# Splitting w_out earlier, its second half in the first half's places, and two row blocks begun ahead

## The chip, the cores and the metric

The kernel runs on one core of a Trainium2 chip. The metric is the device time of one execution in microseconds (us). Engines are named as in the profile: PE (TensorE matmul), PEld (its weight loads), DVE (VectorE), ACT (ScalarE), POOL (GpSimd) and SP (SyncE, which issues most of the DMAs).

## What is computed

One layer of a hybrid trunk over 1152 tokens (1024 latents and 128 context tokens, nine blocks of 128 rows), width 1024. Three mixers work side by side on parts of one input projection: a Fourier mixer (256 columns), an mLSTM (384) and an S5 scan whose output goes through a GLU (384). Their outputs are laid side by side, 1024 wide, and multiplied by w_out (1024 x 1024); then come a gated residual, a norm, a SwiGLU feed-forward layer and a last norm. Cut to what matters here:

```python
out = jnp.concatenate([f_out, m_out, s_out], axis=-1) @ p["w_out"]
x = x + g1 * out
xn = rmsnorm(x, p["norm2_w"]) * (1 + sc2) + sh2
ff = (jax.nn.silu(xn @ p["w_gate"]) * (xn @ p["w_up"])) @ p["w_down"]
```

## The kernel before, in words

**Products in three.** Each large product is made of three PE instructions (`mm3`, L243): both operands are cut into a high part (a copy that ACT rounds, `split`, L264) and a low part (the difference, made by DVE or POOL). A weight must be loaded, copied by ACT and subtracted by DVE or POOL before PE can use it.

**The order of the work.** Streams (Python generators) hand out instructions. `Weaver.run` (L200) holds a model of each engine's clock and, when the program is built, always emits the instruction that can start earliest by that model; between equal ones the stream's number decides, the lower first. A step marked `VP` goes to DVE or POOL, whichever would end first by the model. So every engine's queue has a fixed order, made from estimated costs, and a stream that waits for a name in `done` waits only for that name's instructions to be emitted. All compute instructions have the line L146 (`emit`), so the trace is read by tiles.

**The output projection.** w_out is used in eight units, each the rows of two of the eight 128-row parts (k) and 512 of the columns: units 0 to 3 make the first half of the columns (j = 0), units 4 to 7 the second (j = 1). `raw_feed` (L1426) loads a unit (512 KB) into one of two buffers `fraw`, `wout_feed` (L1436) splits it into a place `wo0` to `wo7`. Places 0 and 1 are in the pool woA, which is there from the GLU on; 2 to 4 are in woM, opened when the Fourier stream is done; 5 to 7 in woB, opened when the mLSTM's `front` stream and the first half's evacuation (`x0evac`) are done, in the room that these leave. Both streams are added only there where the mLSTM chunks start (L1958 and L1959), behind the GLU and the mLSTM states. After w_out, the two buffers take the feed-forward weights.

`out_project` (L1454) goes through j = 0 and then j = 1. For a row block c, `begin(c)` does the Fourier and GLU parts (k = 0 to 4, 15 PE instructions), and the rest of the block does the mLSTM parts (k = 5 to 7, 9 instructions) when chunk c of the mLSTM has given its output (`m{c}`). In the first half `begin(c + 1)` stands ahead of the rest of block c, so that PE has work while a chunk is made; the last block has none behind it. In the second half the blocks go one after another. One block takes one of the eight PSUM banks from its begin to its evacuation (`evac_x0`, L1519, and `evac_x1`, L1538).

Beside it run `mlstm_front` (L1331) and `mlstm_back` (L1370), chunk by chunk: loads of q, k, v and of a broadcast row `nb`; a mask; exponentials on ACT; products on PE; a norm; a transpose; and the split into MT. The GLU (`glu`, L1116), the mLSTM states (`mlstm_states`, L1175) and the Fourier mixer (`fourier`, L1214, `v_store`, L1291) come before or overlap.

After the second half's blocks, the norm (`norm_scale`, `norm_turned`, `norm_h0`, `norm_h1`, L1555 to L1607) makes operands for the Strassen products of the feed-forward layer. `new` (L1615) and `unit_of` (L1571) put these operands (T1 to T4 and b22) into the places 0 to 7 that w_out has left.

Of the kernel before, what the change touches and what calls it, by code (L numbers as in the profile page):

```python
# [111 lines left out]
class Weaver:  # L112
# [47 lines left out]
    def has(self, *names):  # L160
        return lambda: all(n in self.done for n in names)
# [59 lines left out]
def tile_trunk(ctx, tc, I, O, dbg=None):  # L221
# [13 lines left out]
    def pool(stack, name, bufs=1, side=None):  # L235
        return Pool(wv, stack.enter_context(tc.tile_pool(name=name, bufs=bufs, side=side, reuse_waits="tile")), bufs)
# [1054 lines left out]
    def v_store(fp):  # L1291
        wv.fed["pv"] = [[], 0]
        for _ in range(8):
# [3 lines left out]
            give(pv)  # L1297
            yield Q.dma_start(v_d[:, cl], vt)

    MF = []  # L1300
    sg = ctx.enter_context(ExitStack())
    gp = pool(sg, "glu")
    with ExitStack() as sy:
        yp = pool(sy, "yT")
        add("gluw", glu_weights(gp, yp), 3)
        add("yTfeed", glu_load(yp), 4)
        add("glufeed", glu_feed(yp), 5)
        add("glu", glu(gp), 6)
        add("prep", mlstm_prep(pool(sy, "prep")), 4)
        run("proj", "ada")  # L1310
        swb.close()
        sada.close()

        so_, sf_ = ctx.enter_context(ExitStack()), ctx.enter_context(ExitStack())
        L5["woA"] = pool(so_, "woA", side="right")
        four = pool(sf_, "four", side="right")
        add("vstore", v_store(four), 28)
        add("fourier", fourier(four), 30)
        run("prep", "glufeed")
# [103 lines left out]
    ssh = const.tile([128, 2, NT], F32, name="ssh")  # L1423
    Y, YP, R2 = {}, [], {}

    def raw_feed():  # L1426
        yield has("araw1")

        def make(src):
            raw = raws.tile([128, 1024], F32, name="fraw")  # L1430
            yield Q.dma_start(raw.rearrange("p (k c) -> p k c", k=2) if len(src.shape) == 3 else raw, src)
            return raw
        yield from feed("fraw", [I["w_out"][2 * k:2 * k + 2, :, 512 * j:512 * j + 512].rearrange("k p c -> p k c") for j in range(2) for k in range(4)] + [I[n][i, h].rearrange("p k d j -> p (k d j)") for i in range(NG)
                    for n in ("w_gate", "w_up") for h in range(2)], make, RAWS)

    def wout_feed():  # L1436
        def make(u):
            raw = yield from take("fraw")
            if u >= WOA:
                yield has("woB" if u > WOM else "woM")  # L1440
            t = wo_unit(u, f"wo{u}")
            hi, lo = t[:, 0:D], t[:, D:2 * D]
            yield from split(raw, hi, lo, VP)
            used("fraw")
            return [x.rearrange("p (k c) -> p k c", k=2) for x in (hi, lo)]
        return feed("wout", range(8), make, 8)


    def wo_unit(k, name):
        p = L5["woA" if k < WOA else "woB" if k > WOM else "woM"]  # L1450
        return p.tile([128, 2 * D], F32R, name=name, tag=f"wo{k}")


    def out_project():  # L1454
        for j in range(2):
            ws, po = [], {}

            def mm(c, ks):
                b, i = divmod(c, 3)
                cs = slice(i * 128, (i + 1) * 128)  # L1460
                for k in ks:
                    if len(ws) <= k // 2:
                        ws.append((yield from take("wout")))
                    m = [(MF[b][n][:, (k + 2) % 5] if k < 5 else MT[b][n][:, k - 5])[:, cs] for n in range(2)]
                    w = [x[:, k % 2] for x in ws[k // 2]]
                    yield mm3(po[c], *m, *w, k == 0, k == 7)
                    if c == 8 and k % 2:
                        done.add(f"wo{4 * j + k // 2}")
                    if j and c == 8 and k == 4:
                        done.add("obf")  # L1470

            def begin(c):
                yield lambda c=c: len(MF) > c // 3
                po[c], = yield from bank([128, 512], keep=0 if j else 2)
                yield from mm(c, range(3))
                yield has(f"mf{c // 3}")
                yield from mm(c, range(3, 5))
            if j == 0:
                yield has("vstore")
                yield from begin(0)  # L1480
            for c in range(NT):
                if j:
                    yield from begin(c)
                elif c + 1 < NT:
                    yield from begin(c + 1)
                yield has(f"m{c}")
                yield from mm(c, range(5, 8))
                x1_banks[c, j] = po.pop(c)
                if j and c % 3 == 2:
                    done.add(f"ob{c // 3}")  # L1490
        done.add("out")

    def halved(c, j):
# [75 lines left out]


    def unit_of(i, name):  # L1571
        yield has(f"wo{i}")
        return wo_unit(i, name).rearrange("p (k t) -> p k t", k=4)


# [31 lines left out]
    def norm_h1():  # L1607
        yield has("norm_h0")
        KS = range(4)
        part = {q: [[u[:, k] for u in Y[q]] for k in KS] for q in ("11", "21")}  # L1610

        def f(q, k):
            return [u.bitcast(F32) for u in part[q][k]]

        def new(q, *at):  # L1615
            us = []
            for n, i in enumerate(at):
                us.append((yield from unit_of(i, f"{q}{n}")))
            Y[q] = us
            part[q] = [[u[:, k] for u in us] for k in KS]  # L1620
        b12 = []
        for k in KS:
            b12.append((yield from take("nx")))
            d = xw.tile([128, 512], F32, name="xd", bufs=2)
            yield tt(VP, d, b12[k], f("11", k)[0], ALU.subtract)
            yield tt(VP, d, d, f("11", k)[1], ALU.subtract)
            if k == 0:
                yield from new("T1", 0, 1)
            yield from split(d, *part["T1"][k], VP)
        done.add("T1")  # L1630
        b22 = None
        for k in KS:
            yield has(f"b22{k}")
            b22 = L5["b22"]
            if k == 0:
                yield has("obf")
                Y["22"] = [unit("f", 2, n, "y2", (4, 512)) for n in range(2)]
            yield from split(b22[:, k], *[u[:, k] for u in Y["22"]], VP)
        done.add("22")

        for k in KS:
            yield tt(VP, b12[k], b22[:, k], b12[k], ALU.subtract)
            d = xw.tile([128, 512], F32, name="xd", bufs=2)
            yield tt(VP, d, b12[k], f("11", k)[0], ALU.add)
            yield tt(VP, d, d, f("11", k)[1], ALU.add)
            if k == 0:
                yield from new("T2", 5, 6)
                yield from new("T3", 3, 4)
            yield from split(d, *part["T2"][k], VP)
            yield from split(b12[k], *part["T3"][k], VP)  # L1650
            yield tt(VP, b12[k], f("21", k)[0], d, ALU.subtract)
            if k == 3:
                done.update(("T2", "T3"))
            yield tt(VP, b12[k], b12[k], f("21", k)[1], ALU.add)
        yield from new("T4", 7, 2)
        for k in KS:
            yield from split(b12[k], *part["T4"][k], VP)
        done.add("T4")
# [11 lines left out]
    NG = NFF // 2  # L1670
    WOA, WOM = 2, 4
    GROUPS = [(0, 3), (3, 6), (6, 9), (9, 11)]


# [272 lines left out]
    with ExitStack() as sm_:  # L1947
        mw = pool(sm_, "mw")

        for n, shape, k in (("mt0", [128, 3, 128], 1), ("mt1", [128, 3, 128], 1), ("og", [128, 3, 128], 2), ("nu0", [128, H, 97], 1),  # L1950
                            ("nu1", [128, H, 97], 1), ("h", [128, H, 96], 2), ("xh", [128, 512], 3), ("gt", [128, 512], 2), ("g1", [128, 512], 1),
                            ("va", [128, H, 97], 3), ("qc", [96, H, 128], 3), ("kc", [96, H, 128], 2), ("nb", [128, H, 128], 2),
                            ("P0", [128, H, 128], 2), ("P1", [128, H, 128], 2)):
            mw.place(shape, F32, n, k)
        add("front", mlstm_front(mw), 0)
        add("xhfeed", xh_feed(mw), 19)
        add("x0evac", evac_x0(mw), 9)
        add("fraw", raw_feed(), 24)  # L1958
        add("woutfeed", wout_feed(), 25)  # L1959
        add("out", out_project(), 40)  # L1960
        run("fourier")
        sf_.close()
        L5["woM"] = pool(so_, "woM", side="right")
        done.add("woM")
        run("front", "x0evac")
# [394 lines left out]
```

## Time and profile before

| | |
|---|---|
| median of 3 runs | 1444.98 us (1444.38 to 1445.21) |
| the profiled execution's own time | 1445.23 us |
| its span in the trace | 1443.4 us |
| PE busy | 1350.3 us (94% of the span), granted clock 0.973 in the mean |
| PEld busy | 1113.9 us (77%) |
| DVE, ACT, POOL busy | 941.0 us (65%), 532.3 us (37%), 260.6 us (18%) |
| DMA queue of SP | 116180 packets, 195.44 MB |

The span is the time between the first and the last instruction that the profiler saw; the execution's own time is 1.8 us longer, for what lies around it. A busy PE is not PE at its best: its instructions overlap (a row's duration is longer than the distance to the next start), and its clock has two levels, 1.2 and 2.4 GHz; a granted clock of 1.00 means 2.4 GHz for the whole stretch, 0.5 would be 1.2. In a timeline row the bracket tells how long the engine stood before the instruction, and which instruction's end let it go on. A DMA-issuing instruction is listed under SPq; its data land later.

### The profile page before, as it was taken

How to read it: one execution, taken by the hardware profiler on the slowest of the kernel's cores; microseconds unless marked ns; L12 is line 12 of the kernel's file. 1: busy time of each engine (PE TensorE's matmuls, PEld its weight loads, DVE VectorE, ACT ScalarE, POOL GpSimd, SP SyncE). 2: the span in 40 equal slices, each digit the busy share in tenths (PEclk: the TensorE clock that was granted, in tenths of full speed). 3: DMA queues.
4: the chain of work that ended last, by engine and by line, in shares of the span. 5: the costliest groups of instructions: out<-in, count | busy, mean ns of one | idle time of the engine just before them, and what ended most of it. 6: DMA issues, size and time to landing. Idle time of an engine off the chain costs nothing.

```text
span 1443.4 us, 19010 instructions
## 1 busy us (share of the span) xinstructions
PE 1350.3 (94%) x6885; PEld 1113.9 (77%) x6885; DVE 941.0 (65%) x1798; ACT 532.3 (37%) x1059; POOL 260.6 (18%) x342
## 2 busy tenths in 40 slices
PE   6899999997989889879999999999999999999996
PEld 1787788963968678658788888888888877888885
DVE  5957788975134477736876667766567665535897
ACT  2632232443254443314633333223333324443433
POOL 4364556632215101100000000000000010000011
PEclk9999999998999989989999999999999999999999
DMA  9265422255433865143122222322323339735472
GB/s 325 92 180 147 166 87 82 70 173 169 141 99 96 240 184 168 65 168 118 52 86 81 79 98 89 115 96 72 101 79 115 116 133 379 269 112 195 157 240 95
DMA packets 117682, 199.49 MB, mean 138 GB/s; under 512 B 12364, under 2 KB 53684, under 8 KB 117588
## 3 DMA queue, kind: packets, MB, share of 16 engines
q1 hardware_dynamic: 116180, 195.44, 41.2%
q0 software_dynamic: 1408, 2.83, 0.6%
q8 instruction: 54, 0.88, 0.3%
q14 instruction: 40, 0.33, 0.1%
HBM read 151.77 MB, written 46.47 MB: 137 GB/s over the span
## 4 chain that ended last, share of the span: by engine, by line
PE 71%; DVE 12%; DMA 7%; ACT 3%; issue 3%; POOL 2%; SPq 1%; DVEq 0%; POOLq 0%; ACTq 0%
PE bank L146 71%; DMA fraw<-in_w_ada_dram 3%; DVE xo L146 2%; DMA nb<-nit_d 2%; SPq L146 1%; DVE nu L146 1%; DMA hr<-h_d 1%; DMA v_d<-vt 1%; DVE a L146 1%; DMA out_dram<-cn 1%; DVE bp L146 0%; DVE t L146 0%; ACT P L146 0%; ACT L146 0%; DVE h L146 0%
## 5 line engine op out<-in xcount | busy, mean ns | idle before, releaser
L146 PE MATMUL bank<-ow,oh 128*128 128x512 f32 x912 | 212.9, 393 | 6.0 <-DVE ow L146 5.7
L146 PEld LDWEIGHTS bank<-ow,oh 128*128 128x128 f32 x912 | 172.5, 190 | 43.8 <-DVE ow L146 5.1
L146 PE MATMUL bank<-T,sh 128*128 128x512 f32 x480 | 151.3, 390 | 0.0
L146 DVE TENSOR_TENSOR pu<-pu,bank 128x512 f32<-128x512 f32 x102 | 69.9, 685 | 64.2 <-PE bank L146 64.2
L146 PEld LDWEIGHTS bank<-T,sh 128*128 128x128 f32 x480 | 90.2, 188 | 18.3
L146 POOL TENSOR_TENSOR pu<-pu 128x512 f32<-128x512 f32 x10 | 12.9, 1287 | 475.4 <-DVE pu L146 475.4
L146 PE MATMUL bank<-T,sl 128*128 128x512 f32 x240 | 93.6, 390 | 0.0
L146 DVE TENSOR_TENSOR oh<-hr,oh 128x1536 fp32r<-128x1536 f32 (+2 forms) x29 | 45.3, 1563 | 72.9 <-ACT oh L146 72.9
L146 DVE TENSOR_TENSOR sl<-fraw,sh 128x512 fp32r<-128x512 f32 x40 | 27.7, 693 | 63.4 <-ACT sh L146 62.9
L146 ACT ACTIVATE oh<-hr 128x1536 fp32r<-128x1536 f32 (+2 forms) x29 | 38.4, 1323 | 81.2 <-PE bank L146 55.6
L146 POOL TENSOR_TENSOR y<-ms,nhalf 128x1 f32<-128x1 f32 (+2 forms) x26 | 23.4, 902 | 247.2 <-DVE ms L146 246.3
L146 ACT ACTIVATE sh<-sd 128x512 fp32r<-128x512 f32 x40 | 25.3, 632 | 100.2 <-DVE sd L146 53.4
L146 ACT ACTIVATE pu<-bank 128x512 f32<-128x512 f32 x44 | 26.4, 599 | 88.5 <-PE bank L146 88.3
L146 PE MATMUL bank<-fraw,sc 128*32 128x512 f32 x160 | 46.6, 650 | 11.1 <-DMA fraw<-in_w_ada_dram 11.0
L146 PE MATMUL bank<-T,r20t 128*128 128x512 f32 x160 | 52.8, 391 | 0.0
L146 PEld LDWEIGHTS bank<-T,sl 128*128 128x128 f32 x240 | 45.1, 188 | 8.6
L146 DVE TENSOR_TENSOR_SCAN xo<-dec,ri 64x296 f32<-64x296 f32 x48 | 45.2, 941 | 1.8 <-POOL ri L146 0.7
L146 PE MATMUL bank<-y211f,r20t 128*128 128x512 f32 x96 | 39.4, 410 | 2.6 <-ACT xr L146 2.6
L146 PE MATMUL bank<-y210f,r20t 128*128 128x512 f32 x96 | 38.3, 399 | 0.0
L146 PE MATMUL bank<-y210f,r21t 128*128 128x512 f32 x96 | 38.0, 396 | 0.0
L146 PE MATMUL bank<-y201f,r10t 128*128 128x512 f32 x96 | 37.9, 395 | 0.0
L146 PE MATMUL bank<-y200f,r11t 128*128 128x512 f32 x96 | 37.4, 390 | 0.0
(604 smaller groups left out, 3718.6 us busy)
## 6 DMA issues: line engine op xcount, KB each, us to landing
fraw<-in_w_ada_dram SPq DMA_DIRECT2D x40, 512.0 KB
hr<-h_d SPq DMA_DIRECT2D x21, 768.0 KB
wp<-in_w_down_dram SPq DMA_DIRECT2D x15, 768.0 KB
fraw<-in_w_gate_dram SPq DMA_DIRECT2D x22, 512.0 KB
fraw<-in_w_up_dram SPq DMA_DIRECT2D x22, 512.0 KB
h_d<-sg SPq DMA_DIRECT2D x36, 256.0 KB
wraw<-in_w_feat_dram SPq DMA_DIRECT2D x14, 512.0 KB
h_d<-hs SPq DMA_DIRECT2D x27, 256.0 KB
```

The lines of the kernel that those rows point to most:

```text
L146: s.call(*s.a, **s.k)
```

## The change

The diff does five things. `raw_feed` and `wout_feed` are added before the Fourier streams, beside the GLU (numbers 24 and 25, the Fourier stream has 30), no longer at the mLSTM chunks, and `raw_feed` no longer waits for the name `araw1`. Units 5, 6 and 7 go into the places 0, 1 and 2 once the first half's last row block has read those (`wo0`, `wo1`, `wo2` in `done`), not into woB. `out_project` begins row blocks 0 and 1 of the second half (`begin(0, 1)` and `begin(1, 1)`) after the last `begin` of the first half and ahead of the mLSTM parts of block 8, and block 2 ahead of the rest of block 0; these keep two banks free as the first half does. The places 5 to 7 are used by T1 and T2 alone. T1, T2 and T4 change places with one another, and a table `FREE` says what each place waits for; b22, in place 2, now waits for the last product of the projection.

```diff
+    UNIT = (0, 1, 2, 3, 4, 0, 1, 2)
+    FREE = ("wo5", "wo6", "wo7", "wo3", "wo4", "woB", "woB", "woB")
+    def wo_unit(k, name):
+        p = L5["woA" if k < 2 else "woB" if k > 4 else "woM"]
+        return p.tile([128, 2 * D], F32R, name=name, tag=f"wo{k}")
...
+    def wout_feed():
+        def make(u):
+            raw = yield from take("fraw")
+            if u > 1:
+                yield has(("woM", "woM", "woM", "wo0", "wo1", "wo2")[u - 2])
+            t = wo_unit(UNIT[u], f"wo{u}")
...
         L5["woA"] = pool(so_, "woA", side="right")
+        add("fraw", raw_feed(), 24)
+        add("woutfeed", wout_feed(), 25)
         four = pool(sf_, "four", side="right")
...
     def raw_feed():
-        yield has("araw1")
...
         def make(u):
             raw = yield from take("fraw")
-            if u >= WOA:
-                yield has("woB" if u > WOM else "woM")
-            t = wo_unit(u, f"wo{u}")
...
+        def begin(c, j):
+            yield lambda c=c: len(MF) > c // 3
+            po[c, j], = yield from bank([128, 512], keep=2 if not j or c < 2 else 0)
+            yield from mm(c, j, range(3))
+            yield has(f"mf{c // 3}")
+            yield from mm(c, j, range(3, 5))
+        def end(c, j):
+            yield has(f"m{c}")
+            yield from mm(c, j, range(5, 8))
+            x1_banks[c, j] = po.pop((c, j))
...
+        yield has("vstore")
+        yield from begin(0, 0)
+        for c in range(NT):
+            if c + 1 < NT:
+                yield from begin(c + 1, 0)
+            else:
+                yield from begin(0, 1)
+                yield from begin(1, 1)
+            yield from end(c, 0)
+        for c in range(NT):
+            if c in (0, 3, 4, 5, 6, 7, 8):
+                yield from begin(max(c, 2), 1)
+            yield from end(c, 1)
...
     def unit_of(i, name):
-        yield has(f"wo{i}")
+        yield has(FREE[i])
...
-                yield from new("T1", 0, 1)
+                yield from new("T1", 6, 7)
...
-                yield from new("T2", 5, 6)
+                yield from new("T2", 5, 0)
...
-        yield from new("T4", 7, 2)
+        yield from new("T4", 1, 2)
...
         add("x0evac", evac_x0(mw), 9)
-        add("fraw", raw_feed(), 24)
-        add("woutfeed", wout_feed(), 25)
         add("out", out_project(), 40)
```

## Rows read from the trace of the kernel before

**Rows 1.** Stretches: length, then busy time of each engine (instructions), PE clock, DMA share, GB/s

```profile
398.00:477.00 79.00, 73.13 (x369) 62.28 (x370) 33.03 (x82) 36.90 (x71) 30.94 (x35) 0.96 0.39 96
477.00:530.00 53.00, 40.25 (x245) 34.51 (x243) 32.08 (x71) 24.92 (x73) 2.89 (x3) 0.87 0.78 235
530.00:602.00 72.00, 68.48 (x402) 59.22 (x403) 55.83 (x135) 28.53 (x117) 8.02 (x7) 0.98 0.48 146
611.30:620.50 9.20, 5.92 (x19) 4.10 (x18) 4.31 (x8) 1.24 (x3) 0.00 (x0) 0.79 0.18 59
620.50:635.60 15.10, 7.46 (x22) 5.65 (x23) 5.04 (x6) 3.67 (x5) 0.00 (x0) 0.78 0.81 287
635.60:683.00 47.40, 46.61 (x222) 38.43 (x221) 25.03 (x59) 16.61 (x33) 2.82 (x4) 1.00 0.32 114
697.00:730.00 33.00, 30.44 (x142) 24.97 (x140) 26.67 (x42) 17.35 (x34) 0.00 (x0) 0.95 0.12 39
```

**Rows 2.** Timeline of PE: start, duration, instruction, and what it stood for

```profile
494.95 0.50 PE L146 MATMUL bank<-wo,mf00f 128*128 128x512 f32 x1 [2.95 <-DVE wo L146]
...
613.37 0.52 PE L146 MATMUL bank<-ident,h 128*128 128x128 f32 x3 [2.07 <-DVE h L146]
615.09 0.76 PE L146 MATMUL bank<-wo,mt20t 128*128 128x512 f32 x1 [1.20 <-ACT mt20t L146]
...
623.65 0.50 PE L146 MATMUL bank<-wo,mf00f 128*128 128x512 f32 x1 [3.15 <-DVE wo L146]
...
631.20 0.80 PE L146 MATMUL bank<-wo,mt00t 128*128 128x512 f32 x1 [4.50 <-DVE wo L146]
```

**Rows 3.** Timeline of PE, three products at either level of the clock

```profile
633.08 0.63 PE L146 MATMUL bank<-wo,mt01t 128*128 128x512 f32 x1
633.50 0.63 PE L146 MATMUL bank<-wo,mt00t 128*128 128x512 f32 x1
...
640.19 0.39 PE L146 MATMUL bank<-wo,mf00f 128*128 128x512 f32 x1
640.42 0.39 PE L146 MATMUL bank<-wo,mf01f 128*128 128x512 f32 x1
```

**Rows 4.** Timeline of ACT and DVE: the split of unit 7

```profile
628.83 1.06 ACT L146 ACTIVATE wo<-fraw 128x1024 fp32r<-128x1024 f32 x1 [5.55 <-DMA fraw<-in_w_out_dram]
...
629.92 1.22 DVE L146 TENSOR_TENSOR wo<-fraw,wo 128x1024 fp32r<-128x1024 f32 x1 [5.20 <-ACT wo L146]
```

**Rows 5.** The chain of work that ended last, 477 to 565: start, length, what

```profile
487.14 8.31 DMA nb<-nit_d
...
496.23 1.15 DVE wo L146
497.43 3.50 PE bank L146 x19
...
504.90 6.90 DMA nb<-nit_d
...
516.18 4.82 DMA nb<-nit_d
```

**Rows 6.** DMA view of 477 to 500: all packets, and w_out's loads

```profile
DMA packets 5826, 6.82 MB, mean 296 GB/s; under 512 B 395, under 2 KB 3467, under 8 KB 5825
...
fraw<-in_w_out_dram SPq DMA_DIRECT2D x4, 512.0 KB
```

**Rows 7.** Timeline of DVE and POOL in the GLU's stretch

```profile
471.08 0.56 DVE L146 TENSOR_TENSOR Cst<-dc,Cst 96x388 f32<-96x388 f32 x1 [0.18 <-POOL dc L146]
...
472.51 1.00 POOL L146 TENSOR_TENSOR mf21f<-so,mf20f 128x384 fp32r<-128x384 f32 x1
472.58 1.34 DVE L146 TENSOR_TENSOR Cst<-dc,Cst 96x388 f32<-96x388 f32 x1 [0.94 <-POOL dc L146]
```

**Rows 8.** Timeline of PE: the projection's last product, transposes of rows 4 to 7

```profile
682.77 0.39 PE L146 MATMUL bank<-wo,mt20t 128*128 128x512 f32 x1
...
691.17 1.26 PE L146 MATMUL bank<-ident,xr 128*128 128x128 f32 x10
```

More of the change, by code (lines that the diff above doesn't have):

```diff
@@ L1298, in v_store, with raw_feed, make @@
             yield Q.dma_start(v_d[:, cl], vt)
+    NG = NFF // 2
+    UNIT = (0, 1, 2, 3, 4, 0, 1, 2)
[3 more added lines that the diff above has]
+        return p.tile([128, 2 * D], F32R, name=name, tag=f"wo{k}")
+    def raw_feed():
+        def make(src):
+            raw = raws.tile([128, 1024], F32, name="fraw")
+            yield Q.dma_start(raw.rearrange("p (k c) -> p k c", k=2) if len(src.shape) == 3 else raw, src)
+            return raw
+        yield from feed("fraw", [I["w_out"][2 * k:2 * k + 2, :, 512 * j:512 * j + 512].rearrange("k p c -> p k c") for j in range(2) for k in range(4)]
+                        + [I[n][i, h].rearrange("p k d j -> p (k d j)") for i in range(NG) for n in ("w_gate", "w_up") for h in range(2)], make, RAWS)
+    def wout_feed():
[4 more added lines that the diff above has]
+            t = wo_unit(UNIT[u], f"wo{u}")
+            hi, lo = t[:, 0:D], t[:, D:2 * D]
+            yield from split(raw, hi, lo, VP)
+            used("fraw")
+            return [x.rearrange("p (k c) -> p k c", k=2) for x in (hi, lo)]
+        return feed("wout", range(8), make, 8)
     MF = []
@@ L1424, in tile_trunk @@
     Y, YP, R2 = {}, [], {}
-    def raw_feed():
-        yield has("araw1")
[L1429 to L1434, printed above, removed]
@@ L1436, in wout_feed @@
-    def wout_feed():
-        def make(u):
-            raw = yield from take("fraw")
-            if u >= WOA:
-                yield has("woB" if u > WOM else "woM")
-            t = wo_unit(u, f"wo{u}")
[L1442 to L1451, printed above, removed]
@@ L1454, in out_project @@
-    def out_project():
[L1455 to L1490, printed above, removed]
@@ new lines, in out_project, with mm @@
+    def out_project():
+        ws, po = ([], []), {}
+        def mm(c, j, ks):
+            b, i = divmod(c, 3)
+            cs = slice(i * 128, (i + 1) * 128)
+            for k in ks:
+                if len(ws[j]) <= k // 2:
+                    ws[j].append((yield from take("wout")))
+                m = [(MF[b][n][:, (k + 2) % 5] if k < 5 else MT[b][n][:, k - 5])[:, cs] for n in range(2)]
+                w = [x[:, k % 2] for x in ws[j][k // 2]]
+                yield mm3(po[c, j], *m, *w, k == 0, k == 7)
+                if c == 8 and k % 2:
+                    done.add(f"wo{4 * j + k // 2}")
+                if j and c == 8 and k == 4:
+                    done.add("obf")
+        def begin(c, j):
[8 more added lines that the diff above has]
+            x1_banks[c, j] = po.pop((c, j))
+            if j and c % 3 == 2:
+                done.add(f"ob{c // 3}")
+        yield has("vstore")
[11 more added lines that the diff above has]
+            yield from end(c, 1)
@@ L1668, in norm_p @@
             yield from split(t, *[y[:, k0:k0 + 2] for y in YP], VP)
-    NG = NFF // 2
-    WOA, WOM = 2, 4
     GROUPS = [(0, 3), (3, 6), (6, 9), (9, 11)]
```

## The prediction

> **What bounds the kernel now.** I read the page first (PE is busy 94% of the span), then a table of stretches to find where it is not, then the timeline of PE for what it stood for there, then the chain of work that ended last. Between 398 and 730 us PE is nearly full in most stretches [rows 1]: 68.5 of 72 us while the middle mLSTM chunks run, 46.6 of 47.4 us in the projection's second half. Two stretches are poor. From 477 to 530 us it is busy for 40.3 of 53 us, at a clock of 0.87, while the DMA engines are 78% busy. From 611.3 to 635.6 us, the change from the first half of w_out to the second, it is busy for 5.9 of 9.2 and 7.5 of 15.1 us, at 0.79 and 0.78. The reader is to see in the PE timeline that five stands there belong to this part of the program [rows 2]: 2.95 us for the low part of the first w_out unit, 3.15 and 4.50 us for low parts of later units, and 2.07 + 1.20 us for the last chunk's own chain (its transpose and its first split).
>
> **The last chunk and the change of halves.** From the end of block 7's last product (611.3) to 635.6 us are 24.3 us. In them PE runs 3 transposes and 37 products (9 of block 8, 24 of block 0 in the second half, the first 4 of block 1). At the high clock products start 0.23 us apart (640.19 and 640.42), at the low one 0.42 us (633.08 and 633.50) [rows 3]. 37 x 0.227 + 0.4 for the transposes = 8.8 us are needed, so 15.5 us are lost: 10.9 in the four stands above (2.07 + 1.20 + 3.15 + 4.50), the other 4.6 to the low clock and small gaps.
>
> After the change:
> - Units 5 and 6 no longer wait for woB. Their places come free with the products k = 1 and k = 3 of block 8's begin, which run at 602 to 604 us, and their data can be in the buffers since unit 4's split. One split costs 1.06 us on ACT and 1.22 us on DVE [rows 4], so both are ready by about 608. The stand of 3.15 us goes.
> - Unit 7 waits for place 2, free with the first three of block 8's nine products. Behind them stand the other six, begin(2, 1) and k = 5 of block 0, 24 products or 5.4 us, against 1.06 + 1.22 = 2.3 us of split. The stand of 4.50 us goes, if the load was issued in time; it is queued on SP once unit 5's split frees a buffer.
> - begin(0, 1) and begin(1, 1) are 30 products, 6.8 us. They stand behind block 7's rest, so they fill 611.3 to 618.1 us, past the 615.1 at which block 8's first part is ready. The stands of 2.07 and 1.20 us go; block 8 ends some 2 to 3 us later than now, and so do its evacuation, the closing of the pools and the loads of the rows x1. These are next in line, but PE can go on without them: blocks 0 to 2 hold three of eight banks.
> - The two splits cost something beside the chain of chunks 7 and 8: 2 x 1.22 us on DVE, in the order in which DVE works off that chain. I take half, 1.2 us; between 0 and 2.4.
> - The clock is low at 611 and PE has then worked for some 4 us, so part of the 4.6 us stays; I take 1.0.
>
> Gain 15.5 - 1.2 - 1.0 = 13.3 us; at least 8.5 (the early blocks bring nothing: 7.65 of stands and the 2 us of the low clock behind 631.20, less 1.2), at most 15.5.
>
> The 47.4 us behind it [rows 1] are full of PE work and stay as they are, only earlier. The row blocks' evacuations come at the same distance, and DVE is busy for 25 of 47.4 us there.
>
> **The first units, 477 to 530 us.** Four loads of 512 KB stand in the 23 us in which 6.82 MB pass at 296 GB/s [rows 6]; they are 2.1 MB or 7.1 us of that. The chain of waits goes through those DMAs: a row `nb` takes 8.31 us from its issue, right behind the w_out loads, where the next two take 6.90 and 4.82 [rows 5]. Then the chain takes the low part of unit 1 on DVE (1.15) and 3.50 us of PE, in which the first begin was late. With the units loaded and split before, I take 8.31 - 5.9 (the mean of the two) = 2.4 for the load, 1.15 for the split and 1.5 of the 3.5 for PE, 5.0 us. At least 1.2 (only the split goes), at most 8 (8.31 - 4.82 + 1.15 + 3.5). It carries on because the next 72 us are full of PE work [rows 1]. Unit 2 still waits for woM, so the stand in front of it, near 530 us, stays.
>
> **What moves into the GLU's stretch.** Two splits (2 x 1.06 us on ACT, 2 x 1.22 on DVE or longer on POOL) and four loads, two of them ahead of the Fourier constants on SP, two behind a buffer that the splits free. DVE is busy for 33 and ACT for 37 of 79 us there, and DMA 39% [rows 1], so most of it hides; without that cover it is 2 x 2.28 = 4.6 us. Nothing is removed there, so no gain. DVE can be held by POOL: the same instruction takes 0.56 us alone and 1.34 when it starts 0.07 us behind a POOL instruction of 1.00 [rows 7], 0.78 more. I take 1.0 us; between 0 and 4.6.
>
> The Trainium skill speaks against this part (SBUF — State Buffer, Who interferes with whom): a DVE instruction with two SBUF inputs and a POOL instruction that reads SBUF use one port pair, and whoever comes second waits for the whole of the other. Rows 7 agree, a wait of about what was left of POOL's instruction. By that rule each of the two low parts could hold POOL for 1.22 us, 2.4 us for both in place of the 1.0 taken, and the sum would be 1429.3 and not 1427.9.
>
> **Places.** T1 and T2 in woB cost nothing: woB is open before the norm begins. b22 now waits for the projection's last product (682.77), but the transposes that make it run at 691 us [rows 8], 8 us behind.
>
> **The sum.** 1445.23 (the profiled execution's own time, 0.25 above the median of the runs; its span is 1443.4) - 13.3 - 5.0 + 1.0 = 1427.9, so 1428 us. The bounds give 1445.2 - 8.5 - 1.2 + 4.6 = 1440 and 1445.2 - 15.5 - 8 = 1421.7. The plan is made anew from 398 us on, and steps may fall elsewhere by a few us.
>
> **Rivals.**
> - *The early blocks find no banks or come too late.* They need a third idle bank; blocks 7 and 8 and the chunk's products hold some. Then 7.65 + 2.0 - 1.2 = 8.5 us of the change of halves remain: 1445.2 - 8.5 - 5.0 + 1.0 = 1432.7. For it: eight banks serve three streams. Against it: at 611 us DVE has little to do (4.3 of 9.2 us) and evacuates block 7 at once.
> - *The norm does not follow.* The x1 rows are loaded only after block 8's first half is stored, and from 697 to 730 us DVE is busy for 26.7 of 33 us while PE stands for 2.6 [rows 1]. If the norm starts when its loads allow, up to 5 us come back there: 1433. Against it: the full 47.4 us lie between.
> - *Slower: SP stands in the GLU's stretch.* The third w_out load waits on SP for a buffer that a low part on DVE frees, and behind it wait the loads and stores of the Fourier mixer and the states' inputs, on the chain. A stand of s us costs s less some 17 gained: slower from s = 17, by over 0.2% from s = 20, and 1449 at s = 21. Against it: the split needs 2.3 us and DVE is more than half idle there.
> - *It does not do what it says:* the planner leaves the splits and the begins about where they are, since they yield to others; then 1443 to 1447.
>
> **How the numbers follow.** A measurement can tell 0.2% (2.9 us) from no change. Forecast 0.67, no early blocks 0.13, norm 0.10, no effect 0.05, SP 0.05. So faster 0.90, same 0.05, slower 0.05. The range, 1420 to 1438, takes in the forecast's bounds but their last corner, and the first two rivals.
>
> **What would show it.** Right: the stands on low parts of w_out at 495 and at the change of halves are gone, products of the second half stand between the last chunk's products, the clock there is near 1.00, nb lands sooner, PE's 47.4 us come about 17 us earlier and the shift holds at 730. Wrong: a stand of PE on wo or mt of over 3 us after block 7, more PE idle between 398 and 477 than the 5.9 us now, or a wait of the norm that takes the shift back before 730.

## The result and the profile after

The changed kernel takes 1424.99 us (median of 4 runs, 1422.86 to 1427.28) against 1444.68 for the kernel before, beside which it ran (median of 4, 1440.40 to 1445.21): a ratio of 0.9864, 95% interval 0.9838 to 0.9890, so 15.9 to 23.4 us less. A second set, beside other runs of the kernel before, gave 1425.20 us and 0.9857 (0.9834 to 0.9880). The forecast was 1428.0 us, 17.0 below the median of before as it stood then (1444.98).

The profiled execution took 1422.86 us, its span is 1421.1 us, 22.3 less than the one of before. Not all of that is the change's. The first product with `y21t`, in the GLU, starts at 396.93 us and not at 400.07, though PE does the same instructions up to there in both kernels; over the 14 profiled executions of this study it starts between 395.84 and 403.98. So every distance below is counted from that product, which I call G.

| from G, against before (us) | the changed kernel | again | what the prediction had |
|---|---|---|---|
| first product of the mLSTM chunks | +1.40 | +0.78 | +1.0 (GLU stretch) |
| rest of block 1 | -11.57 | -12.47 | |
| rest of block 6 | -3.84 | -4.55 | -4.0 (first units, less the GLU) |
| rest of block 7 | -0.43 | -1.27 | -2.8 (two splits more) |
| rest of block 8 | +3.77 | +2.78 | |
| last product of the projection | -15.97 | -17.22 | -17.3 |
| first product of the last stage (w_down) | -15.38 | -16.51 | -17.3 |
| from there to the end of the span | -3.78 | -3.80 | 0 |

The table of stretches of the changed kernel, as [rows 1], with bounds at points of the program: the GLU's stretch; the first units up to the end of unit 2's stand; the middle chunks up to the start of PE's stand before chunk 7's transposes (530.23 to 604.56 in before, 74.3 us); block 7's rest to block 8's; the second half.

```profile
394.86:475.26 80.40, 75.51 (x375) 63.29 (x376) 35.38 (x85) 39.32 (x74) 32.54 (x36) 0.96 0.47 125
475.26:516.10 40.84, 32.46 (x203) 29.03 (x201) 20.58 (x47) 17.81 (x50) 3.74 (x3) 0.87 0.80 228
516.10:598.62 82.52, 77.00 (x452) 66.53 (x452) 65.31 (x158) 35.53 (x140) 7.43 (x7) 0.96 0.45 138
603.34:615.72 12.38, 12.38 (x42) 9.73 (x43) 4.23 (x11) 2.37 (x11) 1.01 (x1) 0.74 0.16 44
615.72:663.66 47.94, 47.91 (x227) 39.55 (x226) 26.75 (x57) 18.36 (x36) 3.57 (x3) 1.00 0.54 179
```

The 53 us of the first units have become 40.8. The middle, which the prediction took over unchanged, has become longer, 82.5 us against 74.3. Between block 7's rest and block 8's PE now has 42 instructions and no idle time, but a clock of 0.74; from block 8's rest to the projection's end it is full at 1.00.

The timeline of PE of the changed kernel, the stands that answer to [rows 2], and the first product of block 3 in the second half (645.63 before):

```profile
516.10 0.50 PE L146 MATMUL bank<-wo,mf00f 128*128 128x512 f32 x1 [2.35 <-DVE wo L146]
...
601.62 0.52 PE L146 MATMUL bank<-ident,h 128*128 128x128 f32 x3 [3.00 <-DVE r L146]
603.34 0.79 PE L146 MATMUL bank<-wo,mt20t 128*128 128x512 f32 x1 [1.20 <-ACT mt20t L146]
...
627.28 0.39 PE L146 MATMUL bank<-wo,mf10f 128*128 128x512 f32 x1
```

The 2.95 us before unit 0 are gone, so are the 3.15 and 4.50 us for low parts and the 2.07 + 1.20 us in block 8's chain. Unit 2's stand is still there, 11 us sooner counted from G. The stand before chunk 7's transposes, 0.62 us in before, is 3.00 us. From block 7's rest to block 3 of the second half it took 38.72 us (606.91 to 645.63) and takes 23.94 (603.34 to 627.28): 14.8 less.

### The profile page after: what moved, and what is told of

Its sections match the earlier page's. It is cut to its first block, busy times and chain, and to the rows that moved or that the text cites. A ratio compares the mean times of both kernels' runs of the same rounds, so it can differ in the third digit from the quotient of the medians.

```text
span 1421.1 us, 19015 instructions
## 1 busy us (share of the span) xinstructions
PE 1345.3 (95%) x6885; PEld 1111.9 (78%) x6885; DVE 940.3 (66%) x1798; ACT 531.5 (37%) x1059; POOL 263.1 (19%) x342
## 3 DMA queue, kind: packets, MB, share of 16 engines
q0 software_dynamic: 1408, 2.83, 0.7%
## 4 chain that ended last, share of the span: by engine, by line
PE 60%; DVE 5%; ACT 2%; DMA 2%; issue 1%; POOL 1%; SPq 0%; DVEq 0%; POOLq 0%; ACTq 0%
PE bank L146 60%; DVE nu L146 1%; DMA v<-v_d 1%; DMA out_dram<-cn 1%; DMA g<-g_d 0%; POOL dc L146 0%; ACT nu L146 0%; DVE ow L146 0%; DVE acc L146 0%; DVE h L146 0%; ACT P L146 0%; DVE Cst L146 0%; DMA v_d<-vt 0%; DVE P L146 0%; DVE r L146 0%
```

## Experiments

All runs' points, counted as in the table above (start minus that run's own G, minus the same of before); the last column is the distance itself.

| run | block 1 | block 6 | block 7 | block 8 | projection's end | last stage | its start to the end |
|---|---|---|---|---|---|---|---|
| before | 0 | 0 | 0 | 0 | 0 | 0 | 254.16 |
| changed | -11.57 | -3.84 | -0.43 | +3.77 | -15.97 | -15.38 | 250.38 |
| changed, again | -12.47 | -4.55 | -1.27 | +2.78 | -17.22 | -16.51 | 250.36 |
| feeds alone | -14.00 | -6.61 | -6.61 | -6.73 | -7.04 | -6.99 | 256.14 |
| feeds late | -0.81 | -0.40 | +2.90 | +7.01 | -13.00 | -12.30 | 250.35 |
| T4 as before | -12.65 | -4.92 | -1.45 | +2.76 | -17.24 | -16.46 | 256.77 |
| none ahead | -10.93 | -2.97 | +0.27 | -0.13 | -10.23 | -11.56 | 250.36 |
| POOL lows | -12.27 | -4.02 | +2.15 | +4.82 | -14.93 | -14.12 | 251.80 |
| no lows | -12.78 | -5.12 | -4.65 | -3.08 | -22.01 | -21.17 | 250.35 |
| no masks | -8.03 | -6.45 | -4.24 | -0.22 | -19.60 | -17.65 | 251.93 |
| two ahead | -7.79 | +12.96 | +14.02 | +17.54 | -5.24 | -3.30 | 251.69 |
| one sooner | -12.50 | -2.83 | +1.05 | +2.57 | -19.68 | -18.11 | 250.32 |
| one sooner, again | -12.27 | -4.23 | -0.72 | +0.86 | -21.52 | -17.99 | 251.73 |
| T places alone | -1.27 | -1.40 | -1.40 | -2.26 | -3.45 | -3.41 | 253.03 |

How far this repeats: "changed", "again" and "T4 as before" have one order of instructions and agree within 1.4 us up to the last stage; "T places alone" has the order of before up to there and lies up to 3.5 us from it. Each row is one execution, so a difference of this size between two rows is firm only where it repeats, or where a stand or the clock shows where it comes from.

### Which part brings what

**The early feeds alone** (the kernel before, with its own places and order; `raw_feed` no longer waits for `araw1`):

```diff
         L5["woA"] = pool(so_, "woA", side="right")
+        add("fraw", raw_feed(), 24)
+        add("woutfeed", wout_feed(), 25)
...
         add("x0evac", evac_x0(mw), 9)
-        add("fraw", raw_feed(), 24)
-        add("woutfeed", wout_feed(), 25)
```

> The kernel before with one part of the change: w_out's loads and splits begin beside the GLU, places and order of the row blocks as before. Theory (the mLSTM chain gives it back): PE comes to unit 2 some 12 us sooner, counted from the first mLSTM product, as in the changed kernel (36.0 there, 48.4 before), but from there to block 7's rest it takes some 10 us longer than before (76.7 before, 87.2 changed), and the GLU's stretch costs 1.4. Sum -0.4 us, so 1443 to 1446 us, a ratio of 0.999 to 1.001, and block 7's rest no more than 2 us sooner. Rival 1 (the prediction's term): 5.0 less 1.0 are kept, 4 us, a ratio of 0.997. Rival 2 (what is given back comes from the splits of units 5 and 6 ahead of chunk 7, which this kernel doesn't have): 6 us or more are kept, a ratio of 0.996 or less.

Measured: 1441.16 us, a ratio of 0.9974 (0.9953 to 0.9996), 0.6 to 6.8 us less. By the trace 14.0 us are gained at block 1's rest, 6.6 are left at block 6's and stay. My theory falls: what the mLSTM chain takes back, 7.4 us, leaves half standing, and the further loss of the changed kernel between blocks 6 and 7 isn't here. The time is rival 1's (0.997); the trace keeps more, 7.0 us, and gives 2.0 back in the last stage. PE's stands at the change of halves are:

```profile
607.60 0.87 PE L146 MATMUL bank<-ident,h 128*128 128x128 f32 x3 [2.07 <-DVE h L146]
609.67 0.79 PE L146 MATMUL bank<-wo,mt20t 128*128 128x512 f32 x1 [1.21 <-ACT mt20t L146]
618.53 0.50 PE L146 MATMUL bank<-wo,mf00f 128*128 128x512 f32 x1 [3.17 <-DVE wo L146]
625.49 0.80 PE L146 MATMUL bank<-wo,mt00t 128*128 128x512 f32 x1 [3.90 <-DVE wo L146]
```

They are the four of [rows 2] again, 10.4 us in sum: the early feeds do nothing for this place.

**The places and the order, with late feeds** (the changed kernel):

```diff
     def raw_feed():
+        yield has("araw1")
...
-        add("fraw", raw_feed(), 24)
-        add("woutfeed", wout_feed(), 25)
         four = pool(sf_, "four", side="right")
...
+        add("fraw", raw_feed(), 24)
+        add("woutfeed", wout_feed(), 25)
         add("out", out_project(), 40)
```

> The changed kernel, but w_out's loads and splits begin only where the mLSTM chunks start, as before. Theory: the early start is worth about nothing (-12.4 + 10.6 + 1.4 = -0.4 us), so this kernel has the whole gain of the change within 1.5 us, a ratio of 0.986 to 0.989 to before; PE comes to unit 2 late (48 us behind the first mLSTM product) and still does block 7's rest within 2 us of the changed kernel's. Rival (the prediction's terms): 4 us are missing, a ratio of 0.990.

Measured: 1430.34 us, 0.9900 (0.9878 to 0.9922). In the trace 3 to 4 us are missing at the projection's end (-13.00 against -15.97 and -17.22). That is no more than two executions of one order can differ by, but the time agrees (all five runs, 1428.36 to 1431.58 us, lie above the changed kernel's two medians), and so does what the early feeds bring alone. The rival was right, and with it the prediction's 4 us for this part.

**No row block begun ahead**:

```diff
-            else:
-                yield from begin(0, 1)
-                yield from begin(1, 1)
             yield from end(c, 0)
+        for c in range(2):
+            yield from begin(c, 1)
```

> The changed kernel without the two row blocks begun ahead: begin(0, 1) and begin(1, 1) stand behind the rest of block 8. Theory: the new places take away the stands on low parts of w_out, 7.65 us, but the two stands in block 8's own chain return (2.07 + 1.20 us before) and with them most of the low clock there (4.6 us before), so it is 4 to 8 us slower than the changed kernel, a ratio of 0.990 to 0.992 to before. Rival 1: the early begins do nothing that the units' being ready doesn't do alone; within 1.5 us of the changed kernel. Rival 2: more than 8 us are lost, since units 5 and 6 then come no sooner than they are needed.

Measured: 1427.36 us, 0.9874 (0.9852 to 0.9897); 2.2 to 2.4 us above the changed kernel's medians where the theory had 4 to 8; the time alone can't tell the two apart. In the trace 5.7 to 7.0 us are missing at the projection's end, as the theory had it, and 3.8 to 5.0 at the last stage. The two stands in block 8's own chain are back (1.34 + 1.21 us), and from block 7's rest to block 8's the clock is the low one throughout:

```profile
604.34:612.12 7.78, 5.24 (x12) 3.26 (x12) 3.70 (x11) 2.36 (x11) 1.01 (x1) 0.50 0.10 36
```

### What the middle chunks go by

In the chain of waits of the changed kernel from 564 to 585 us there is no PE instruction. It goes round in the mLSTM's own steps on DVE and ACT; these are some of one round:

```profile
568.23 0.56 DVE h L146
568.87 1.19 ACT nu L146 x8
570.25 0.96 ACT P L146 x3
571.85 0.68 DVE nb L146
573.94 0.68 DVE P L146
576.47 0.53 ACT mt10t L146
577.03 0.56 DVE mt11t L146
577.59 0.54 DVE nu L146
579.40 0.56 DVE nu L146
580.48 0.56 DVE h L146
```

From `h` to `h` it is 12.25 us. The kernel before comes to the same pace once its backlog on PE is worked off: block 5's rest to block 6's takes 12.39 us there (584.49 to 596.88).

**The masks left out** (one step of that round):

```diff
-                yield tt(VP, nb, nb, masks[d].unsqueeze(1).to_broadcast([128, H, 128]), ALU.add)
```

> The changed kernel, but the masks of the mLSTM chunks are left out (the row nb goes to the exponentials as it was loaded; two DVE instructions of 0.68 us less in each chunk, one of which stands in the chain of waits). Theory (from 540 to 600 us the chunks go at the pace of their own chain on DVE and ACT, 12.3 us each, and PE waits): a chunk takes 0.7 to 1.4 us less, the rest of block 6 comes 3 to 6 us sooner behind the rest of block 1, and the projection ends 3 to 6 us sooner. Rival (PE's work or the loads set the pace): the rest of block 6 moves by less than 1 us.

Measured: 1419.91 us, 0.9841 (0.9807 to 0.9874). From block 3's rest to block 6's three chunks take 33.79 us (553.72 to 587.51) against 37.10 (552.80 to 589.90): 1.1 us less for each. From block 1's rest to block 6's it is 52.40 us against 58.55, 6.2 less, though the plan put block 1 itself 3.5 to 4.4 us later; at the projection's end 2.4 to 3.6 us are left, about the lower end of what was expected. The theory holds: the chain on DVE and ACT sets the pace there.

### The two splits in chunk 7's chain

Units 5 and 6 are split where their places come free, beside block 8's begin. The timelines of ACT and DVE of the changed kernel:

```profile
594.85 1.06 ACT L146 ACTIVATE wo<-fraw 128x1024 fp32r<-128x1024 f32 x1 [3.22 <-PE bank L146]
595.82 0.26 ACT L146 ACTIVATE nu<-h 128x96 f32<-128x96 f32 x1
...
598.56 1.23 DVE L146 TENSOR_TENSOR wo<-fraw,wo 128x1024 fp32r<-128x1024 f32 x1 [1.31 <-ACT wo L146]
599.71 0.15 DVE L146 TENSOR_TENSOR t<-y 128x4 f32<-128x4 f32 x1
```

`h` was ready at 594.65 (594.10 + 0.55), its squares on ACT start at 595.82, behind a high part; the norm's `t`, whose input POOL had made by 598.40 (597.39 + 1.01), starts at 599.71, behind a low part. From block 6's rest to block 7's all four kernels with these splits on DVE and the changed plan up to there take 3.2 to 3.5 us longer than before (columns of blocks 6 and 7). Of this 2.4 us are the stand before chunk 7's transposes, 3.00 us in all of them; in before it is

```profile
605.18 0.52 PE L146 MATMUL bank<-ident,h 128*128 128x128 f32 x3 [0.62 <-DVE r L146]
```

The other 0.9 to 1.1 us come ahead of both splits: block 6's nine products run at the low clock, as the stretches from block 6's rest to block 8's begin show, of before and then after, each with 11 instructions on PE:

```profile
596.88:599.20 2.32, 2.32 (x11) 1.78 (x11) 1.94 (x6) 0.21 (x1) 0.00 (x0) 1.00 0.29 85
```

```profile
589.90:593.29 3.39, 3.39 (x11) 2.69 (x11) 2.02 (x5) 0.21 (x1) 0.00 (x0) 0.60 0.18 53
```

The evacuation `gt` on DVE waits for these products (0.86 us, at 593.49), and `h` stands behind it, so this delay goes into chunk 7's chain too.

**Their low parts left out**:

```diff
-            return [x.rearrange("p (k c) -> p k c", k=2) for x in (hi, lo)]
+            return [x.rearrange("p (k c) -> p k c", k=2) for x in ((hi, hi) if u in (5, 6) else (hi, lo))]
```

and for these units `split` is the copy on ACT alone.

> The changed kernel, but the low parts of units 5 and 6 are left out: PE reads the high part in their place, so the products are as many, and only the two DVE instructions of 1.22 us are gone. Theory (the splits stand in the chain of chunk 7 with both parts, the high ones on ACT ahead of the squares and the low ones on DVE ahead of the rows of the norm): about 1.2 to 2.4 of the 3.3 us that block 7's rest comes late go, and the projection ends 1 to 2 us sooner. Rival 1: the low parts are all of it, 3 us or more go. Rival 2: ACT's high parts are all of it, nothing changes (under 0.5 us).

Measured: 1421.58 us, 0.9857 (0.9825 to 0.9888), an interval too wide to tell. In the trace the loss between blocks 6 and 7 falls from 3.3 or 3.4 to 0.5 us, and the projection ends 4.8 to 6.0 us sooner than in the changed kernel. The figure is near rival 1's, but 1.1 us of it is block 6's rest, which ran at the high clock in this execution; the stand before chunk 7's transposes falls from 3.00 to 1.15 us, 1.85 less, as the theory had it, and 0.5 more than in before is left for the high parts on ACT. That the gain goes on behind block 7 no expectation had. Block 6's rest to block 7's in the changed kernel (block 7's to block 8's is the row 603.34:615.72 of its table above), then both stretches without the low parts and the stand between them:

```profile
589.90:603.34 13.44, 9.24 (x46) 7.58 (x45) 9.63 (x25) 4.70 (x17) 1.01 (x1) 0.88 0.31 111
```

```profile
592.54:603.04 10.50, 8.14 (x46) 6.65 (x45) 7.07 (x23) 4.64 (x16) 1.01 (x1) 1.00 0.41 139
603.04:612.79 9.75, 9.66 (x42) 7.71 (x43) 4.75 (x13) 2.43 (x11) 1.01 (x1) 1.00 0.19 60
```

```profile
601.28 0.55 PE L146 MATMUL bank<-ident,h 128*128 128x128 f32 x3 [1.15 <-DVE h L146]
```

The same 42 instructions take 12.38 us at a clock of 0.74 and 9.75 at 1.00. So two instructions of 1.22 us cost 1.9 us as a stand before chunk 7's transposes, and 2.6 more go with the low clock behind the long stand. That clock isn't a loss against before, where block 7's nine products were slow too (the last starts 3.77 us behind the first there, 3.74 in the changed kernel, 2.33 here).

**The low parts on POOL**:

```diff
-            yield from split(raw, hi, lo, VP)
+            yield from split(raw, hi, lo, P_ if u in (5, 6) else VP)
```

> The changed kernel, with the low parts of units 5 and 6 made by POOL (it works for about 1 us in each 12 there) and not by DVE. Theory: the two lows on DVE, 1.22 us each, stand in the chain of chunk 7 and are most of the 3.3 us by which block 7's rest comes later behind block 6's than before; without them 1.5 to 2.4 us of that come back and the projection ends as much sooner. Rival (the port that DVE and POOL share): POOL's instruction takes some 2.7 us (an estimate from the 1.00 us that 384 columns took, times 1024/384) and DVE's of the chain wait for it, and the chain's own small POOL instruction waits behind it; block 7's rest comes 1 to 4 us later than in the changed kernel.

Measured: 1425.55 us, 0.9871 (0.9848 to 0.9893). Block 6's rest to block 7's takes 6.2 us more than before, 2.8 more than with the low parts on DVE (the stand before chunk 7's transposes is 5.59 us); the rival was right. By the projection's end 1.0 to 2.3 us of it are left, and the time is the changed kernel's. The timelines of POOL and DVE:

```profile
596.44 2.38 POOL L146 TENSOR_TENSOR wo<-fraw,wo 128x1024 fp32r<-128x1024 f32 x1 [12.39 <-ACT wo L146]
599.05 2.34 POOL L146 TENSOR_TENSOR wo<-fraw,wo 128x1024 fp32r<-128x1024 f32 x1 [0.24 <-ACT r L146]
601.35 1.01 POOL L146 TENSOR_TENSOR y<-ms,nhalf 128x4 f32<-128x4 f32 x1
```

```profile
597.45 1.39 DVE L146 TENSOR_SCALAR ms<-s 128x4 f32<-128x4 f32 x1 [1.77 <-ACT nu L146]
599.07 2.35 DVE L146 TENSOR_TENSOR r<-r,flr 128x4 f32<-128x4 f32 x1 [0.23 <-ACT r L146]
```

`ms` takes 0.16 us in the changed kernel and `r` 0.15; here both last until POOL's instruction ends (598.8 and 601.4), and the chain's own POOL instruction `y` waits behind the second. The Trainium skill has this rule (SBUF — State Buffer, Who interferes with whom: whoever comes second on the port pair that DVE and POOL share waits for the whole of the other), and the trace agrees for `r`, which reads two tensors: an instruction of four columns waits as a long one would. `ms`, which reads one, was held too.

### Begins sooner

**One step sooner**:

```diff
             else:
-                yield from begin(0, 1)
                 yield from begin(1, 1)
+                yield from begin(2, 1)
+            if c + 2 == NT:
+                yield from begin(0, 1)
             yield from end(c, 0)
         for c in range(NT):
-            if c in (0, 3, 4, 5, 6, 7, 8):
-                yield from begin(max(c, 2), 1)
+            if c > 2:
+                yield from begin(c, 1)
```

In `begin`, `keep=2` then holds for the second half's blocks below 3.

> The changed kernel, with each early row block of the second half one step sooner: begin(0, 1) ahead of block 7's rest, begin(1, 1) and begin(2, 1) ahead of block 8's. Theory: from 560 to 615 us the mLSTM's own chain of DVE and ACT sets the end and PE stands for 3.0 + 1.2 us in front of block 7's rest; begin(0, 1), 3.4 us of products, fills that stand, block 8's rest comes when it comes now (within 1 us), and the projection ends 2 to 4 us sooner, 0.1 to 0.3% below the changed kernel. Rival: PE takes its instructions in order, so the products begun there push chunk 8's behind them; block 8's rest comes 2 to 4 us later and nothing is gained, within 0.1%.

Measured: 1419.54 us, 0.9822 (0.9798 to 0.9846), beside the changed kernel's 1425.20 and 0.9857. It was run again:

> The kernel with each early row block one step sooner, once more, to see whether its lead over the changed kernel repeats. If it does: a ratio of 0.981 to 0.984 to before, the projection's end 2 to 4 us sooner than in the changed kernel, counted from the first product of the GLU's stretch. If the lead was chance: 0.986.

Measured: 1419.72 us, 0.9837 (0.9808 to 0.9867). By the traces it is 2.5 to 5.6 us ahead of the changed kernel at the projection's end, in every pairing of the executions, and still 1.5 to 2.7 at the last stage; where the rest goes in between wasn't tried. Beside each other the medians are 5.7 us apart; by the ratio of the second set it is 0.20%, 2.9 us. It is the fastest version of the study that computes all, though the intervals of the two ratios beside each other still overlap. The stretches from block 6's rest to 7's, to 8's and to block 3 of the second half (second execution):

```profile
590.47:604.01 13.54, 12.24 (x60) 10.12 (x59) 9.80 (x25) 4.69 (x17) 1.01 (x1) 0.92 0.33 109
604.01:613.77 9.76, 9.66 (x43) 7.71 (x43) 4.16 (x11) 2.37 (x11) 1.01 (x1) 1.00 0.18 54
613.77:622.59 8.82, 8.45 (x37) 6.68 (x36) 2.52 (x3) 1.79 (x3) 0.00 (x0) 1.00 0.40 119
```

Chunk 7's chain takes as long as in the changed kernel (13.54 against 13.44 us), but PE does 60 instructions in it and not 46; the stand of 3.00 us is filled, the clock behind it is 1.00, and block 7's rest to block 8's takes 9.76 us and not 12.38. The theory had the gain; that about half of it comes by the clock it didn't say.

**Two row blocks ahead all through** (`keep=2` and the second half's loop as one step sooner):

```diff
         yield from begin(0, 0)
+        yield from begin(1, 0)
         for c in range(NT):
-            if c + 1 < NT:
-                yield from begin(c + 1, 0)
+            if c + 2 < NT:
+                yield from begin(c + 2, 0)
             else:
-                yield from begin(0, 1)
-                yield from begin(1, 1)
+                yield from begin(c + 2 - NT, 1)
+            if c + 1 == NT:
+                yield from begin(2, 1)
             yield from end(c, 0)
```

> The changed kernel, with two row blocks begun ahead all through: begin(c + 2) ahead of the rest of block c in the first half, begin(0, 1) ahead of block 7's rest, begin(1, 1) and begin(2, 1) ahead of block 8's. Block 8 has then read units 0 and 1 some 10 us sooner, and units 5 and 6 are split sooner. Theory (the chain of DVE and ACT sets the pace of the chunks, 12.3 us each, and PE only fills): block 6's rest comes as now, PE's busy time from 540 to 615 us rises by 3 to 6 us, and the projection ends by as much sooner, 0.2 to 0.4% below the changed kernel. Rival 1: a bank more is held, the chunks' products find none, and the chain slows; block 6's rest comes 2 us or more later and the time is the same or longer. Rival 2: the two splits only fall into another chunk's chain; block 8's rest as now, gain under 1 us.

Measured: 1437.03 us, 0.9945 (0.9927 to 0.9962), 12 us slower than the changed kernel. Block 6's rest comes 17 us later. The chain of waits from 565 us on shows why:

```profile
564.64 14.88 PE bank L146 x64
...
584.38 8.50 PE bank L146 x30
...
601.64 7.57 PE bank L146 x28
```

The chain now goes through PE, for up to 64 instructions in one piece: the chunk's own small products stand behind begun row blocks in PE's fixed order. The clock there is low as well: 0.69 from 565 to 580 us and 0.79 from 580 to 612. Rival 1 had the loss; that a missing bank causes it isn't shown, and PE's order and clock can account for it without one, though none of the three was tried apart.

### The places of T1 to T4

Between the first product of the last stage and the end the changed kernel is 3.8 us shorter, with the same products. PE's timeline of before has a second stand there, which the changed kernel has not:

```profile
1189.24 5.49 PE L146 MATMUL bank<-ow,oh 128*128 128x512 f32 x12 [2.74 <-DVE ow L146]
1196.13 2.97 PE L146 MATMUL bank<-ow,oh 128*128 128x512 f32 x12 [1.41 <-DVE ow L146]
```

```profile
1170.72 5.97 PE L146 MATMUL bank<-ow,oh 128*128 128x512 f32 x24 [2.70 <-DVE ow L146]
1176.53 2.20 PE L146 MATMUL bank<-ow,hp 128*128 128x512 f32 x9
```

The SP queue's rows around it, of before and then after:

```profile
1180.85 0.92 SPq L146 DMA_DIRECT2D wp<-in_w_down_dram  x2
1181.82 1.28 SPq L146 DMA_DIRECT2D hr<-h_d  x2
```

```profile
1152.72 3.09 SPq L146 DMA_DIRECT2D wp<-in_w_down_dram  x2
1161.89 0.91 SPq L146 DMA_DIRECT2D hr<-h_d  x2
```

The first w_down tile of the last stage lies, in the memory's layout, over the second and third places that woB hands out: 6 and 7 in before, 7 and 5 in the changed kernel, which takes place 6 first (worked out from the program; the waits of `wp` agree). In before place 7 held T4's high part, which the last product with a T reads (1180.43 us); `wp` waited for it on SP and `hr` behind `wp`. In the changed kernel T1 and T2 lie there, which are done sooner, and T4 is in 1 and 2.

**T4 put back** over that tile, in the changed kernel:

```diff
-                yield from new("T2", 5, 0)
+                yield from new("T2", 1, 0)
-        yield from new("T4", 1, 2)
+        yield from new("T4", 5, 2)
```

> The changed kernel, with T2 in places 1 and 0 and T4 in 5 and 2, so that T4's high part lies again where the first w_down tile of the last stage lies. The order of the instructions is the same on every engine. Theory: the last stage's loads wait again for T4's last product and ACT waits some 4.4 us for a load of the hidden rows, so it is 3.9 us slower than the changed kernel, at a ratio of 0.989 to 0.990 to before; all up to 1150 us stays the same. Rival (the prediction: where T1 to T4 lie costs nothing): the same time as the changed kernel, 0.9864.

Measured: 1430.81 us, 0.9896 (0.9871 to 0.9921). The distances up to the last stage are the changed kernel's; the last stage takes 256.77 us and not 250.4. The chain of waits has the load again, and PE's second stand is 3.64 us:

```profile
1165.84 0.38 SPq L146
1166.28 0.48 SPq L146
1166.81 10.03 DMA hr<-h_d
```

**T1 to T4 moved, and nothing else**, in the kernel before:

```diff
-                yield from new("T1", 0, 1)
+                yield from new("T1", 0, 3)
-                yield from new("T2", 5, 6)
-                yield from new("T3", 3, 4)
+                yield from new("T2", 5, 7)
+                yield from new("T3", 6, 4)
-        yield from new("T4", 7, 2)
+        yield from new("T4", 1, 2)
```

> The kernel before, with nothing changed but the places of T1 to T4 (T1 in 0 and 3, T2 in 5 and 7, T3 in 6 and 4, T4 in 1 and 2), so that no part of T4 lies where the first w_down tile comes; the order of the instructions is the same on every engine. Theory: the last stage's first loads no longer wait for T4's last product; from the first product of the last stage to the end of the span it takes 250 to 252 us (254 to 257 where T4 lies there), so 3 to 6 us less, a ratio of 0.996 to 0.998 to before. Rival (places cost nothing): 1.000, and 254 us or more.

Measured: 1439.13 us, 0.9978 (0.9959 to 0.9998), 0.3 to 5.9 us less. The second stand is gone, but the last stage takes 253.03 us, not 250 to 252; the clock says why. The first 6 us of the last stage, of this kernel and of the changed one:

```profile
1184.27:1190.27 6.00, 6.00 (x14) 4.74 (x15) 6.00 (x7) 1.14 (x3) 0.65 (x2) 0.50 0.96 345
```

```profile
1170.72:1176.72 6.00, 6.00 (x25) 4.72 (x26) 6.00 (x7) 1.13 (x3) 0.65 (x2) 1.00 1.04 362
```

Behind the same stand of 2.7 us PE runs here at 1.2 GHz, there at 2.4, which makes the 2.7 us between 253.03 and 250.36. It isn't the change's: the kernels without T4 over the tile show 250.3, 251.7 to 251.9, and 253.03, and the three with it 254.16, 256.14 and 256.77. The places are worth the second stand, 1.4 to 3.6 us, and the low clock where one follows it: with T4 put back the 12 us from 1180.23 on run at 0.73. Where the clock over the first 6 us is about the same, the runs with T4 over the tile are 1.1 us longer (254.16 to 253.03, at 0.50), 4.2 to 4.5 (256.14, at 0.72) and 6.4 (256.77, at 0.97). Of the 3.8 of the two kernels compared here 1.4 is the second stand, and most of the rest is the clock of their executions: 0.50 in before, 1.00 in the changed kernel.

## Why the prediction was right, step by step

The time came within 3 us and inside the range, closer than the parts of the sum deserve. By its own terms:

- **Change of halves, -13.3.** From block 7's rest to block 3 it is -14.8, where the term without the splits was 15.5 - 1.0 = 14.5: the stands of 3.15, 4.50, 2.07 and 1.20 us went, as forecast, and the last two are back without the early begins. The 1.0 for the clock came too: the 81 products and three transposes from 607.51 to 627.28 took 19.8 us, 1.0 more than at 0.227 us each and 0.4 for the transposes. Units 5 and 6 were split by 599.8 us (608 was forecast), unit 7 hid behind the begins, and the blocks found their banks.
- **"The two splits cost ... I take half, 1.2 us; between 0 and 2.4."** This is the term that was mis-sized: the stand before chunk 7's transposes grew by 2.4 us, twice what I took and at its upper bound. DVE's two instructions are 1.9 of it by the run without them, so most of their length stands in the chain and not half; ACT's two, which I had left out, are some 0.5. A further 0.9 to 1.1 us by which block 7's rest came later had no term in the sum: block 6's rest at the low clock, ahead of the splits.
- **First units, -5.0.** At block 6's rest -3.8 to -4.9, with the GLU's +0.2 to +1.4 in it, as the sum had it (-4.0). But the reason given, "it carries on because the next 72 us are full of PE work", was wrong. The gain was 12 us at block 1, and the mLSTM chain, at 12.25 us a chunk, took 7.7 to 7.9 of it back; the PE work was full in before only because it was behind. I took the size from three small terms and missed both of the large ones, so that the size came out is luck.
- **GLU, +1.0.** The first product of the chunks comes 0.2 to 1.4 us later in all eleven executions with early feeds. SP did not stand: the third and fourth load are issued at 405.98 and 408.12 us. One POOL instruction that started beside a low part on DVE took 1.34 us, the next of its kind 1.00. The 2.4 us that I had worked out from the Trainium skill (SBUF — State Buffer, Who interferes with whom) didn't come, since no more than that one met a low part.
- **Places, "cost nothing".** b22 and woB cost nothing that the shift shows; T4's place brought a second stand of 1.4 to 3.6 us, and low clock behind some of them, some 500 us later, which no row that I had read bore on: I had asked who waits for a place, not what is loaded over it next.
- **Sum and rivals.** -17.3 forecast; by the trace -16.0 to -17.2 at the projection's end, -15.4 to -16.5 at the last stage, and 3.8 more in it, for which the sum had nothing. By the first of these the sum is right within 1.3 us, less than the 3.5 by which two executions of before's order differ. The shift held through the norm: -18.35 us at 627.28, -18.15 at 705.94, by the traces' own clocks. No rival came: banks were there, SP did not stand, and without the early begins the time is 1427.4, not 1432.7.

## To carry to other kernels

Before a stretch "full of PE work" is taken to carry a gain on, look whether PE is the bound there or has only a backlog: an instruction moved into a stretch where another engine's chain sets the pace costs that chain most of its length (here 1.9 of 2.4 us), and TensorE may stand at the low clock behind the longer stand. Work to spare goes where such a stand is: one row block ahead of block 7's rest brought 1.5 to 5.6 us by the traces, one more ahead of every chunk lost 12. When buffers change places, read what is loaded into that memory next, even if that is in another stage.

## What was not expected of the hardware

- After the same PE stand of 2.7 us, at the same instruction, the granted clock over the next 6 us was 1.00 in six of the eleven executions without T4 over the tile (the changed kernel, twice), 0.72 in four and 0.50 in one (1184.27 above); the last stage takes 250.3 to 250.4, 251.7 to 251.9 and 253.03 us.
- After a stand of 1.5 to 1.6 us before chunk 6's transposes the clock over the first 2 us of block 6's rest was 0.50 in eight executions, all of the changed order, and 1.00 in four (before, the early feeds alone, the T places alone, and the changed order without the low parts). Why isn't known.
- A POOL instruction of 2.34 us made a DVE instruction of 0.15 us last 2.35.
- One execution's start, up to G, differs by up to 8.1 us with PE's instructions the same (395.84 to 403.98), more than most parts of this change are worth.
